# The token recurrence's diagonal and first five levels by blocks of 32 tokens instead of 128

## The chip, the core and the metric

The kernel runs on one core of a Trainium2 chip. The metric is the device time of one execution, in microseconds (us). The core works with several engines that run side by side and wait for one another through semaphores: TensorE (PE in the profile; its weight loads are PEld), VectorE (DVE), ScalarE (ACT), GpSimd (POOL) and SyncE (SP), which issues the transfers from memory.

## The reference, cut to what matters

Two layers work on 256 tokens of 1024 features. Each layer has a half-step feed-forward network, a mixer, a cross attention to 256 memory tokens and a second half-step feed-forward network. The mixer joins two groups of heads, and one of them is touched here, a recurrence with 4 heads of key and value dimension 128:

```python
S_t = diag(f_t) S_{t-1} + k_t i_t^T        # k_t = 1 - f_t, per head
o_t = S_t^T q_t
# the same without a state:
a[t, s] = sum_d q[t, d] * k[s, d] * prod_{s < j <= t} f[j, d]      for s <= t
o_t = sum_s a[t, s] * i_s
```

The other group, 8 heads of softmax attention with a decay (FoX), runs in the same mixer and isn't changed.

## The kernel before

Dense projections split every float32 weight into a high and a low part: a DMA brings 1 MB (`raw`), ACT casts it to the high part (`whi`, L149) and DVE subtracts to get the low part (`wlo`, L150). Seven buffers of each part are in use. PE then runs three matmuls per block of weights (L376, L377, L378). Of these, L378 is the one that reads `wlo` where the weights stream through as the stationary side.

`hgrn` computes the matrix `a` above for two tiles of 128 tokens (t = 0, 1) and 4 heads, in PSUM, as keys on the partitions by queries on the free axis. It starts with the diagonal (s = t): for each tile and head one 128 x 128 matmul of `k` with `q` (L577, tile `ad`). DVE multiplies it by the identity into the tile `A` (L579). Then come seven levels. At level `lv` queries in the right half and keys in the left half of a block of 2 * 2^lv tokens meet. `qf` holds q times the product of f from the middle of the block to t, and `k` holds k times the product from s to the middle. After every level DVE multiplies the right halves of `qf` (L612) and the left halves of `k` (L614) by block products `tots` (L618), so that the next level can use them.

Levels 0 to 4 run whole 128 x 128 matmuls, 4 heads for each of the two tiles, so 8 in a level (L604, tile `al`). They compute much that isn't wanted, and DVE takes only the positions of this level into `A` with a mask (`copy_predicated`, L625, one per tile, 4 x 128 columns). Levels 5 and 6 run only the blocks that are wanted (L598): 16 matmuls of 32 x 32 at level 5, 8 of 64 x 64 at level 6, and ACT copies the blocks into `A` (L622). Level 5 writes its blocks to partitions 0 and 64, and so uses two of the four groups of 32 columns of the array.

The matmuls of the recurrence work on float32 operands. In the trace one such matmul shows as two records.

The kernel is written as generators that hand over to each other. Each `yield` gives an estimate of TensorE's time, and a planner (`drive`) takes the next generator whose time has come. So the `fq` and `fk` projections (tile `acc`), the normalisation of the memory tokens (`mem`, `pt`), the gates of FoX (`pc`, `lf`, `fab`, `fe`, `fl`) and the levels of `hgrn` stand between each other on every engine. A scheduler then sets the final order of each engine's queue. Each queue runs in its order.

Of the kernel before, what the change touches and what calls it, by code (L numbers as in the profile page):

```python
# [17 lines left out]
P = 128  # L18
# [6 lines left out]
NT = S // P  # L25
# [20 lines left out]
def hymba_kernel(  # L46
# [13 lines left out]
    sm = ctx.enter_context(tc.tile_pool(name="sm", bufs=4))  # L60
# [18 lines left out]
    def smp(name="smp"):  # L79
        return pss.tile([P, 512], F32, name=nm(name), tag="smp")  # L80
# [101 lines left out]
    def consts_mixer():  # L182
        it = s4([P, P], I32, "it")
        ip = s4([P, P], I32, "ip")
        nc.gpsimd.iota(it, pattern=[[1, P]], base=0, channel_multiplier=0)
        nc.gpsimd.iota(ip, pattern=[[0, P]], base=0, channel_multiplier=1)
        xr = s4([P, P], I32, "xr")
        nc.vector.tensor_tensor(out=xr, in0=it, in1=ip, op=ALU.bitwise_xor)
        xf = s4([P, P], F32, "xf")
        nc.vector.tensor_copy(out=xf, in_=xr)  # L190
        tf = s4([P, P], F32, "tf")
        nc.vector.tensor_copy(out=tf, in_=it)
        pf = s4([P, P], F32, "pf")
        nc.vector.tensor_copy(out=pf, in_=ip)
        up = s4([P, P], F32, "up")
        nc.vector.tensor_tensor(out=up, in0=tf, in1=pf, op=ALU.is_gt)
        nc.vector.tensor_tensor(out=xf, in0=xf, in1=up, op=ALU.mult)
        masks = cp.tile([P, 5, P], U32, name="masks")
        prev = s4([P, P], F32, "ge")
        nc.vector.tensor_scalar(out=prev, in0=xf, scalar1=1.0, scalar2=None, op0=ALU.is_ge)  # L200
        for lv in range(5):
            ge = s4([P, P], F32, "ge")
            nc.vector.tensor_scalar(out=ge, in0=xf, scalar1=float(2 << lv), scalar2=None, op0=ALU.is_ge)
            nc.vector.tensor_tensor(out=masks[:, lv, :], in0=prev, in1=ge, op=ALU.subtract)
            prev = ge
        tri = cp.tile([P, NT, S], F32, name="tri")
        nc.vector.memset(tri[:, 0, :], 1.0)
        nc.vector.memset(tri[:, 1, 0:P], 0.0)
        for t in range(NT):
            nc.vector.tensor_tensor(out=tri[:, t, t * P:(t + 1) * P], in0=tf, in1=pf, op=ALU.is_ge)  # L210
        cmask = cp.tile([P, S], F32, name="cmask")
        nc.vector.memset(cmask[:, 0:P], 0.0)
        nc.vector.tensor_scalar(out=cmask[:, P:S], in0=up, scalar1=NEG, scalar2=None, op0=ALU.mult)


        ge = small(4, "gesel", bufs=2)
        pm = small(1, "pm", bufs=1)
        nc.vector.tensor_scalar(out=pm, in0=pf[:, 0:1], scalar1=64.0, scalar2=-64.0, op0=ALU.is_ge, op1=ALU.mult)
        nc.vector.tensor_tensor(out=pm, in0=pm, in1=pf[:, 0:1], op=ALU.add)
        for j, v in enumerate((8.0, 16.0, 24.0, 32.0)):  # L220
            nc.vector.tensor_scalar(out=ge[:, j:j + 1], in0=pm, scalar1=v, scalar2=None, op0=ALU.is_ge)
        sel = cp.tile([P, 6], F32, name="sel")

        nc.vector.tensor_scalar(out=sel[:, 0:1], in0=ge[:, 0:1], scalar1=-1.0, scalar2=1.0, op0=ALU.mult, op1=ALU.add)
        nc.vector.tensor_tensor(out=sel[:, 1:2], in0=ge[:, 0:1], in1=ge[:, 1:2], op=ALU.subtract)
        nc.vector.tensor_tensor(out=sel[:, 2:3], in0=ge[:, 1:2], in1=ge[:, 3:4], op=ALU.subtract)
        nc.vector.tensor_tensor(out=sel[:, 3:4], in0=ge[:, 2:3], in1=ge[:, 1:2], op=ALU.subtract)
        nc.vector.tensor_tensor(out=sel[:, 4:5], in0=ge[:, 3:4], in1=ge[:, 2:3], op=ALU.subtract)
        nc.vector.tensor_scalar(out=sel[:, 5:6], in0=ge[:, 1:2], scalar1=-1.0, scalar2=1.0, op0=ALU.mult, op1=ALU.add)
        dif = small(8, "dif")  # L230
        nc.vector.tensor_scalar(out=dif, in0=tf[:, 0:8], scalar1=pm, scalar2=-1.0, op0=ALU.subtract, op1=ALU.mult)
        oh = cp.tile([P, 8], F32, name="oh")
        nc.vector.tensor_scalar(out=oh, in0=dif, scalar1=0.0, scalar2=None, op0=ALU.is_equal)
        for v in (8.0, 16.0, 24.0):
            nc.vector.scalar_tensor_tensor(out=oh, in0=dif, scalar=v, in1=oh, op0=ALU.is_equal, op1=ALU.add)
        return masks, tri, cmask, sel, oh


    lbs = cp.tile([P, DEPTH, 4], F32, name="lbs")
# [327 lines left out]

    def hgrn(q, f, k, v, gw, oT, masks, ready, done):
        yield ready
        A2 = s4([P, NT, 4, P], F32, "A")  # L570
        A = [A2[:, t] for t in range(NT)]
        qf = s4([P, 4, S], F32, "qf")
        nc.vector.tensor_tensor(out=qf, in0=q, in1=f, op=ALU.mult)
        for t in range(NT):
            ps = smp("ad")
            for h in range(4):
                nc.tensor.matmul(ps[:, h * P:(h + 1) * P], lhsT=k[:, h, t * P:(t + 1) * P],  # L577
                                 rhs=q[:, h, t * P:(t + 1) * P], start=True, stop=True)
            nc.vector.tensor_tensor(out=A[t], in0=ps.rearrange("p (h t) -> p h t", h=4),  # L579
                                    in1=ident.unsqueeze(1).to_broadcast([P, 4, P]), op=ALU.mult)  # L580
        yield 8 * 0.213
        tots = s4([P, 1024], F32, "tots")
        tot = f.rearrange("p h t -> p (h t)")
        qflat = qf.rearrange("p h t -> p (h t)")
        kflat = k.rearrange("p h t -> p (h t)")
        for lv in range(7):
            hb = 1 << lv
            pss_ = []
            blk = lv >= 5
            if blk:  # L590
                ps = smp("al")
                pss_.append(ps)
                for t in range(NT):
                    for h in range(4):
                        c0 = (4 * t + h) * hb
                        for s0 in range(0, P, 2 * hb):
                            a = t * P + s0
                            nc.tensor.matmul(ps[s0:s0 + hb, c0:c0 + hb], lhsT=k[:, h, a:a + hb],  # L598
                                             rhs=qf[:, h, a + hb:a + 2 * hb], start=True, stop=True)
            else:  # L600
                for t in range(NT):
                    ps = smp("al")
                    for h in range(4):
                        nc.tensor.matmul(ps[:, h * P:(h + 1) * P], lhsT=k[:, h, t * P:(t + 1) * P],  # L604
                                         rhs=qf[:, h, t * P:(t + 1) * P], start=True, stop=True)
                    pss_.append(ps)
            nb = 4 * S // (2 * hb)
            tv = tot.rearrange("p (b two) -> p b two", two=2)
            qv = qflat.rearrange("p (b two j) -> p b two j", two=2, j=hb)
            kv = kflat.rearrange("p (b two j) -> p b two j", two=2, j=hb)  # L610
            with tc.high_priority(offset=HP):
                nc.vector.tensor_tensor(out=qv[:, :, 1, :], in0=qv[:, :, 1, :],  # L612
                                        in1=tv[:, :, 0:1].to_broadcast([P, nb, hb]), op=ALU.mult)
                nc.vector.tensor_tensor(out=kv[:, :, 0, :], in0=kv[:, :, 0, :],  # L614
                                        in1=tv[:, :, 1:2].to_broadcast([P, nb, hb]), op=ALU.mult)
                if lv < 6:
                    nt_ = tots[:, 1024 - 2 * nb:1024 - nb]
                    nc.vector.tensor_tensor(out=nt_, in0=tv[:, :, 0], in1=tv[:, :, 1], op=ALU.mult)  # L618
                    tot = nt_
            if blk:  # L620
                for s0 in range(0, P, 2 * hb):
                    nc.scalar.copy(out=A2[s0:s0 + hb, :, :, s0 + hb:s0 + 2 * hb],  # L622
                                   in_=pss_[0][s0:s0 + hb, 0:8 * hb].rearrange("p (t h j) -> p t h j", t=NT, h=4))
            for t in range(0 if blk else NT):
                nc.vector.copy_predicated(A[t], masks[:, lv, :].unsqueeze(1).to_broadcast([P, 4, P]),  # L625
                                          pss_[t].rearrange("p (h t) -> p h t", h=4))
            yield 8 * 0.107 if blk else 8 * 0.213
            yield (LAT_LVL,)
        ps = smp("ax")
        for h in range(4):  # L630
# [385 lines left out]
```

## Time and profile before

| what | value |
|---|---|
| median of 3 runs | 1259.83 us (1258.87 to 1261.07) |
| profiled execution | 1260.18 us, its span 1258.4 us |
| granted TensorE clock | 0.998 of full |
| PE busy | 1232.6 us (98%) |
| DVE busy | 767.4 us (61%) |
| ACT busy | 624.3 us (50%) |
| POOL busy | 36.3 us (3%) |
| DMA | 221.20 MB, 51.5% of 16 engines' span on the main queue |

Busy time of matmuls counts the length of their pipeline, so a busy PE can still be faster or slower. What tells the cost of a matmul is the step from its start to the start of the next. The stretch in which the levels run is about 256 to 296 us in the first layer, and 617 us later in the second one.

### The profile page before, as it was taken

What the parts mean: (1) busy time and instruction counts of PE and PEld (TensorE: products, weight loads), DVE (VectorE), ACT (ScalarE), POOL (GpSimd) and SP (SyncE); (2) the same over time, 40 slices, a digit from 0 to 9 for tenths busy, and PEclk for the clock granted to TensorE, in tenths of its full rate; (3) what the DMA queues carried; (4) which work ended last, traced back from release to release, by engine and by line L of the source; (5) the groups of instructions that cost most, each with busy time, mean ns of one, the idle gap of its engine ahead of it and who ended that gap; (6) DMA issues with size and microseconds to landing.
All of it is one profiled execution on the core that took longest, in us unless ns stands there. A gap on an engine that the chain in (4) does not pass through costs nothing.

```text
span 1258.4 us, 20147 instructions
## 1 busy us (share of the span) xinstructions
PE 1232.6 (98%) x8393; PEld 1129.2 (90%) x8393; DVE 767.4 (61%) x1117; ACT 624.3 (50%) x927; POOL 36.3 (3%) x50
## 2 busy tenths in 40 slices
PE   5999999999999999999999999999999999999997
PEld 4999988999889889998889998889998898899986
DVE  6554646597865674555474554476886766645643
ACT  5544434556854463444354454265485644544531
POOL 0000000002000000000000000000020000000000
PEclk9999999999999999999999999999999999999999
DMA  8654754635345264556474556465343634555640
GB/s 269 219 201 140 252 181 154 229 92 197 128 173 185 101 223 162 199 172 218 148 239 146 201 185 217 135 218 202 118 139 131 220 117 145 173 201 168 234 167 34
DMA packets 100748, 221.20 MB, mean 176 GB/s; under 512 B 4136, under 2 KB 16688, under 8 KB 100656
## 3 DMA queue, kind: packets, MB, share of 16 engines
q1 hardware_dynamic: 100656, 219.90, 51.5%
q8 instruction: 66, 1.08, 0.3%
q14 instruction: 26, 0.21, 0.1%
HBM read 218.84 MB, written 1.05 MB: 175 GB/s over the span
## 4 chain that ended last, share of the span: by engine, by line
PE 87%; ACT 4%; DVE 4%; DMA 2%; issue 1%; POOL 0%; SPq 0%; POOLq 0%; DVEq 0%; ACTq 0%
PE acc L376 27%; PE acc L377 27%; PE acc L378 27%; DVE wlo L150 2%; DMA mem<-in_mem_dram 1%; PE pt L297 1%; ACT whi L149 1%; ACT pp L711 1%; ACT fqs L727 1%; DMA raw<-in_ffn_w_gate_dram 1%; PE al L604 1%; ACT fks L729 1%; ACT fks L728 0%; POOL mrs L278 0%; PE cpo L377 0%
## 5 line engine op out<-in xcount | busy, mean ns | idle before, releaser
L150 DVE TENSOR_TENSOR wlo<-raw,whi 128x1024 fp32r<-128x1024 f32 x400 | 479.3, 1224 | 323.2 <-ACT whi L149 321.9
L149 ACT CAST whi<-raw 128x1024 fp32r<-128x1024 f32 x400 | 406.5, 1047 | 340.8 <-PE acc L378 180.3
L376 PE MATMUL acc<-xfh,whi 128*128 128x256 f32 x1536 | 433.8, 282 | 0.0
L377 PE MATMUL acc<-xfl,whi 128*128 128x256 f32 x1536 | 431.4, 281 | 0.0
L378 PE MATMUL acc<-xfh,wlo 128*128 128x256 f32 x1536 | 429.3, 280 | 0.0
L377 PEld LDWEIGHTS acc<-xfl,whi 128*128 128x128 f32 x1536 | 290.3, 189 | 0.4
L378 PEld LDWEIGHTS acc<-xfh,wlo 128*128 128x128 f32 x1536 | 289.8, 189 | 0.0
L376 PEld LDWEIGHTS acc<-xfh,whi 128*128 128x128 f32 x1536 | 288.7, 188 | 0.6
L376 PE MATMUL acc<-whi,hth 128*128 128x512 f32 x352 | 138.6, 394 | 0.0
L377 PE MATMUL acc<-wlo,hth 128*128 128x512 f32 x352 | 138.5, 393 | 0.0
L378 PE MATMUL acc<-whi,htl 128*128 128x512 f32 x352 | 138.1, 392 | 0.0
L376 PE MATMUL acc<-whi,xfh 128*128 128x512 f32 (+1 forms) x256 | 94.8, 371 | 1.6 <-ACT xfh L303 1.6
L377 PE MATMUL acc<-wlo,xfh 128*128 128x512 f32 (+1 forms) x256 | 93.9, 367 | 0.0
L378 PE MATMUL acc<-whi,xfl 128*128 128x512 f32 (+1 forms) x256 | 93.8, 366 | 0.0
L378 PEld LDWEIGHTS acc<-whi,htl 128*128 128x128 f32 x352 | 66.2, 188 | 15.1
L376 PEld LDWEIGHTS acc<-whi,hth 128*128 128x128 f32 x352 | 66.1, 188 | 14.9
L377 PEld LDWEIGHTS acc<-wlo,hth 128*128 128x128 f32 x352 | 66.1, 188 | 14.8
L376 PEld LDWEIGHTS acc<-whi,xfh 128*128 128x128 f32 x256 | 48.4, 189 | 10.0 <-ACT xfh L303 2.0
L378 PEld LDWEIGHTS acc<-whi,xfl 128*128 128x128 f32 x256 | 48.3, 188 | 8.8 <-DVE xfl L304 0.6
L284 ACT ACTIVATE jk<-xs 128x512 f32<-128x512 f32 x36 | 21.7, 603 | 68.5 <-DVE xs L478 66.4
L377 PEld LDWEIGHTS acc<-wlo,xfh 128*128 128x128 f32 x256 | 48.3, 189 | 7.8
L303 ACT CAST hth<-sil 128x512 fp32r<-128x512 f32 x36 | 22.3, 621 | 62.2 <-DVE sil L552 62.2
(226 smaller groups left out, 1373.7 us busy)
## 6 DMA issues: line engine op xcount, KB each, us to landing
raw<-in_ffn_w_down_dram SPq DMA_DIRECT2D x44, 1024.0 KB, 4.9
raw<-in_ffn_w_up_dram SPq DMA_DIRECT2D x40, 1024.0 KB, 5.5
raw<-in_ffn_w_gate_dram SPq DMA_DIRECT2D x38, 1024.0 KB, 5.2
raw<-in_w_in_dram SPq DMA_DIRECT2D x24, 1024.0 KB, 5.3
raw<-in_cross_wk_dram SPq DMA_DIRECT2D x8, 1024.0 KB, 6.0
raw<-in_w_out_dram SPq DMA_DIRECT2D x8, 1024.0 KB, 4.9
raw<-in_cross_wv_dram SPq DMA_DIRECT2D x8, 1024.0 KB, 5.1
raw<-in_cross_wq_dram SPq DMA_DIRECT2D x8, 1024.0 KB, 5.5
```

Source lines behind the costliest of these rows:

```text
L149: nc.scalar.copy(out=hi[:, :kk * cw], in_=sl)
L150: nc.vector.tensor_tensor(out=lo[:, :kk * cw], in0=sl, in1=hi[:, :kk * cw].bitcast(F32), op=ALU.subtract)
L284: nc.scalar.activation(dst, half(src, j), AF.Square, scale=1.0 / 32.0, accum_out=ss[:, j:j + 1])
L297: nc.tensor.transpose(pt[:, j * P:(j + 1) * P], hn[:, kt * P:(kt + 1) * P], ident)
L303: nc.scalar.copy(out=hi, in_=src)
L376: nc.tensor.matmul(ps, lhsT=lh, rhs=rh, start=start, stop=False)
L377: nc.tensor.matmul(ps, lhsT=lh, rhs=rl, start=False, stop=False)
L378: nc.tensor.matmul(ps, lhsT=ll, rhs=rh, start=False, stop=stop)
L604: nc.tensor.matmul(ps[:, h * P:(h + 1) * P], lhsT=k[:, h, t * P:(t + 1) * P], rhs=qf[:, h, t * P:(t + 1) * P], start=True, stop=True)
L711: nc.scalar.activation(dst, src, AF.Exp, bias=nmx[:, t:t + 1], scale=scale, accum_out=sms[:, t:t + 1])
L727: nc.scalar.copy(out=qs[own, :, sub, :], in_=qv.unsqueeze(1).to_broadcast([64, 2, S]))
L729: nc.scalar.copy(out=ks[oth, 0, sub, :], in_=kv)
```

## The change

The diagonal and the levels 0 to 4 are computed in blocks of 32 tokens. A helper `blocks` runs, for each tile and head, four matmuls of 128 x 32 keys by 32 queries, which write to partitions 0, 32, 64 and 96: 32 matmuls for the diagonal and 32 for each of the levels 0 to 4. Levels 5 and 6 use the same helper with the same matmuls as before. All 32 blocks lie in 256 columns of one PSUM tile. DVE masks them into a compact tile `Ac` of 8 x 32 columns, one instruction a level in place of two of twice the width. After level 4 ACT copies `Ac` into `A` in four pieces, and since the rest of `A` isn't written by DVE any longer, POOL clears `A` at the start (`memset`). The masks are built for 32 columns, and the estimates in the `yield`s are new: 1.3 in place of 8 * 0.213 for the diagonal and the levels 0 to 4, and 0.8 in place of 8 * 0.107 for levels 5 and 6. Lines of the first part move by 4 and those behind `hgrn` by 2.

```diff
-        masks = cp.tile([P, 5, P], U32, name="masks")
...
+        eye = cp.tile([P, 32], F32, name="eye")
+        nc.vector.tensor_scalar(out=eye, in0=xb[:, 1, :], scalar1=0.0, scalar2=None, op0=ALU.is_equal)
...
+        masks = cp.tile([P, 5, 32], U32, name="masks")
...
         A2 = s4([P, NT, 4, P], F32, "A")
         A = [A2[:, t] for t in range(NT)]
+        nc.gpsimd.memset(A2, 0.0)
+        Ac = sm.tile([P, 8, 32], F32, name=nm("Ac"), tag="Ac", bufs=1)
...
-        for t in range(NT):
-            ps = smp("ad")
-            for h in range(4):
-                nc.tensor.matmul(ps[:, h * P:(h + 1) * P], lhsT=k[:, h, t * P:(t + 1) * P],
-                                 rhs=q[:, h, t * P:(t + 1) * P], start=True, stop=True)
-            nc.vector.tensor_tensor(out=A[t], in0=ps.rearrange("p (h t) -> p h t", h=4),
-                                    in1=ident.unsqueeze(1).to_broadcast([P, 4, P]), op=ALU.mult)
-        yield 8 * 0.213
+        def blocks(ps, rhs, hb, step):
+
+            for t in range(NT):
+                for h in range(4):
+                    c0 = (4 * t + h) * hb
+                    for s0 in range(0, P, hb + step):
+                        a = t * P + s0
+                        nc.tensor.matmul(ps[s0:s0 + hb, c0:c0 + hb], lhsT=k[:, h, a:a + hb],
+                                         rhs=rhs[:, h, a + step:a + step + hb], start=True, stop=True)
+
+        ps = smp("ad")
+        blocks(ps, q, 32, 0)
+        nc.vector.tensor_tensor(out=Ac, in0=ps[:, 0:256].rearrange("p (g t) -> p g t", g=8),
+                                in1=eye.unsqueeze(1).to_broadcast([P, 8, 32]), op=ALU.mult)
+        yield 1.3
...
+            ps = smp("al")
+            blocks(ps, qf, max(32, hb), hb if lv >= 5 else 0)
...
-            for t in range(0 if blk else NT):
-                nc.vector.copy_predicated(A[t], masks[:, lv, :].unsqueeze(1).to_broadcast([P, 4, P]),
-                                          pss_[t].rearrange("p (h t) -> p h t", h=4))
-            yield 8 * 0.107 if blk else 8 * 0.213
+            else:
+                nc.vector.copy_predicated(Ac, masks[:, lv, :].unsqueeze(1).to_broadcast([P, 8, 32]),
+                                          ps[:, 0:256].rearrange("p (g t) -> p g t", g=8))
+            if lv == 4:
+                for s0 in range(0, P, 32):
+                    nc.scalar.copy(out=A2[s0:s0 + 32, :, :, s0:s0 + 32],
+                                   in_=Ac[s0:s0 + 32].rearrange("p (t h) j -> p t h j", t=NT))
+            yield 1.3 if lv < 5 else 0.8
```

The order of the queues changes only around the levels, in the same way in both layers, and SP's queue stays as it is. On PE, before, the `fq` projection of the first layer (tile `acc_2538`) stands after the diagonal and level 0. Its fourth pair of weight buffers, `whi_2524` and `wlo_2525`, is read here, and level 1 (`al_2578`, then `al_2583`) comes only after 30 of these matmuls:

```order
L378 MATMUL acc_2538<-xfh_1883,wlo_2521 128x256
L376 MATMUL acc_2538<-xfh_1883,whi_2524 128x256
L377 MATMUL acc_2538<-xfl_1884,whi_2524 128x256
L378 MATMUL acc_2538<-xfh_1883,wlo_2525 128x256
L376 MATMUL acc_2538<-xfh_1883,whi_2524 128x256
L377 MATMUL acc_2538<-xfl_1884,whi_2524 128x256
L378 MATMUL acc_2538<-xfh_1883,wlo_2525 128x256
...
L378 MATMUL acc_2538<-xfh_1881,wlo_2449 128x256
L604 MATMUL al_2578<-qf_2481,kk_2132 128x128 x4
L604 MATMUL al_2583<-qf_2481,kk_2132 128x128 x4
```

In the changed program the same place on PE has other buffer numbers (`whi_2569` and `wlo_2570` are the fourth pair, `al_2623` is level 1, whose helper's line is L589; L382 is the old L378):

```order
L382 MATMUL acc_2583<-xfh_1882,wlo_2566 128x256
L380 MATMUL acc_2583<-xfh_1882,whi_2569 128x256
L381 MATMUL acc_2583<-xfl_1883,whi_2569 128x256
L589 MATMUL al_2623<-qf_2482,kk_2131 32x32 x17
L382 MATMUL acc_2583<-xfh_1882,wlo_2570 128x256
L380 MATMUL acc_2583<-xfh_1882,whi_2569 128x256
...
L382 MATMUL acc_2583<-xfh_1880,wlo_2448 128x256
L589 MATMUL al_2623<-qf_2482,kk_2131 32x32 x15
L380 MATMUL acc_2583<-xfh_1880,whi_2451 128x256
```

Level 1 begins 10 matmuls earlier, after 20 of the projection, and is cut in two parts of 17 and 15 blocks, with 10 projection matmuls between them. The first reader of `wlo_2570` stands right behind the first part.

On DVE, before, the subtraction that makes `wlo_2525` stands ahead of the diagonal's mask and of the products that level 1 waits for:

```order
L291 TENSOR_SCALAR mem_2414<-mem_2414,mrs_2422 128x512 x2
L839 TENSOR_TENSOR zb_2381<-acc_2382,fb_1953 128x8
L839 TENSOR_TENSOR zb_2381<-acc_2383,fb_1953 128x8
L150 TENSOR_TENSOR wlo_2525<-raw_2384,whi_2524 128x1024
L579 TENSOR_TENSOR A_2480<-ad_2483,ident 128x512
L618 TENSOR_TENSOR tots_2495<-fg_2131 128x512
L579 TENSOR_TENSOR A_2480<-ad_2489,ident 128x512
L612 TENSOR_TENSOR qf_2481<-qf_2481,fg_2131 128x512
L614 TENSOR_TENSOR kk_2132<-kk_2132,fg_2131 128x512
L618 TENSOR_TENSOR tots_2495<-tots_2495 128x256
```

And the same place on DVE in the changed program, from the same normalisation of the memory tokens (`mem`) on:

```order
L295 TENSOR_SCALAR mem_2413<-mem_2413,mrs_2421 128x512 x2
L616 TENSOR_TENSOR tots_2518<-fg_2130 128x512
L594 TENSOR_TENSOR Ac_2481<-ad_2484,eye 128x256
L616 TENSOR_TENSOR tots_2518<-tots_2518 128x256
L841 TENSOR_TENSOR zb_2380<-acc_2381,fb_1952 128x8
L841 TENSOR_TENSOR zb_2380<-acc_2382,fb_1952 128x8
L610 TENSOR_TENSOR qf_2482<-qf_2482,fg_2130 128x512
L612 TENSOR_TENSOR kk_2131<-kk_2131,fg_2130 128x512
L623 COPY_PREDICATED Ac_2481<-masks,al_2519 128x256
L150 TENSOR_TENSOR wlo_2570<-raw_2383,whi_2569 128x1024
L150 TENSOR_TENSOR wlo_2576<-raw_2445,whi_2575 128x1024
L150 TENSOR_TENSOR wlo_2580<-raw_2445,whi_2579 128x1024
```

The subtraction for the fourth pair, now `wlo_2570`, has moved behind the products for level 1 and behind the mask of level 0.

## Rows read from the trace of the kernel before

**Rows 1.** The page: busy time of each engine, and the last chain by engine.

```profile
PE 1232.6 (98%) x8393; PEld 1129.2 (90%) x8393; DVE 767.4 (61%) x1117; ACT 624.3 (50%) x927; POOL 36.3 (3%) x50
...
PE 87%; ACT 4%; DVE 4%; DMA 2%; issue 1%; POOL 0%; SPq 0%; POOLq 0%; DVEq 0%; ACTq 0%
```

**Rows 2.** Busy by stretch: us, PE, PEld, DVE, ACT, POOL, PEclk, DMA, GB/s.

```profile
255.00:304.00 49.00, 48.51 (x446) 47.82 (x445) 41.91 (x75) 23.58 (x47) 4.79 (x7) 1.00 0.43 143
873.00:921.50 48.50, 47.82 (x441) 47.13 (x440) 41.41 (x74) 23.16 (x47) 4.73 (x7) 1.00 0.43 143
```

**Rows 3.** Timeline of PE, diagonal and level 0 (start us, length us, engine, line).

```profile
255.97 0.28 PE L378 MATMUL acc<-whi,xfl 128*128 128x260 f32 x1
256.09 1.95 PE L577 MATMUL ad<-hq,kk 128*128 128x128 f32 x16
257.87 1.95 PE L604 MATMUL al<-qf,kk 128*128 128x128 f32 x16
...
259.90 0.29 PE L378 MATMUL acc<-xfh,wlo 128*128 128x256 f32 x1
```

**Rows 4.** Timeline of PE, levels 5 and 6 of the first layer.

```profile
284.89 0.28 PE L378 MATMUL acc<-xfh,wlo 128*128 128x256 f32 x1
285.10 0.70 PE L598 MATMUL al<-qf,kk 128*32 128x32 f32 x32
...
286.07 0.28 PE L378 MATMUL acc<-xfh,wlo 128*128 128x256 f32 x1
...
289.26 0.28 PE L378 MATMUL acc<-xfh,wlo 128*128 128x256 f32 x1
289.46 1.15 PE L598 MATMUL al<-qf,kk 128*64 128x64 f32 x16
...
290.88 0.28 PE L378 MATMUL acc<-xfh,wlo 128*128 128x256 f32 x1
```

**Rows 5.** The same, narrow windows: the last record of each of the two bursts.

```profile
285.61 0.20 PE L598 MATMUL al<-qf,kk 128*32 128x32 f32 x1
...
290.39 0.22 PE L598 MATMUL al<-qf,kk 128*64 128x64 f32 x1
```

**Rows 6.** Timeline of DVE, first layer, from the product q * f on.

```profile
255.88 1.22 DVE L573 TENSOR_TENSOR qf<-hq,fg 128x1024 f32<-128x1024 f32 x1
...
258.33 0.23 DVE L839 TENSOR_TENSOR zb<-acc,fb 128x8 f32<-128x8 f32 x2
258.48 1.22 DVE L150 TENSOR_TENSOR wlo<-raw,whi 128x1024 fp32r<-128x1024 f32 x1
259.61 0.69 DVE L579 TENSOR_TENSOR A<-ad,ident 128x512 f32<-128x512 f32 x1
...
262.01 0.69 DVE L614 TENSOR_TENSOR kk<-kk,fg 128x512 f32<-128x512 f32 x1
262.61 0.42 DVE L618 TENSOR_TENSOR tots<-tots 128x256 f32<-128x256 f32 x1
262.95 1.35 DVE L625 COPY_PREDICATED A<-masks,al 128x512 f32<-128x512 uint32 x2
...
270.53 0.50 DVE L684 SCALAR_TENSOR_TENSOR lf<-zb,fl 128x128 f32<-128x128 f32 x2
```

**Rows 7.** Timeline of ACT, first layer: gates of FoX, and a wait further on.

```profile
268.06 0.21 ACT L679 ACTIVATE fe<-fab 128x16 f32<-128x16 f32 x1 [7.59 <-DVE fab L677]
268.18 0.58 ACT L789 ACTIVATE fq<-acc 128x512 f32<-128x512 f32 x1
268.78 1.28 ACT L681 ACT_TABLE_LOAD   x1
...
286.05 1.05 ACT L149 CAST whi<-raw 128x1024 fp32r<-128x1024 f32 x1 [4.63 <-DMA raw<-in_cross_wk_dram]
```

**Rows 8.** Timeline of PE, first layer: the matmul that waits for the gates.

```profile
270.98 1.10 PE L690 MATMUL pc<-tri,lf 128*128 128x256 f32 x4 [0.49 <-DVE lf L684]
```

**Rows 9.** The chain that ended last, where the levels have ended.

```profile
303.65 0.45 PE hot L664 x4
```

More of the change, by code (lines that the diff above doesn't have):

```diff
@@ L186, in consts_mixer @@
         nc.gpsimd.iota(ip, pattern=[[0, P]], base=0, channel_multiplier=1)
[L187 to L190, printed above, removed]
         tf = s4([P, P], F32, "tf")
@@ L196, in consts_mixer @@
         nc.vector.tensor_tensor(out=up, in0=tf, in1=pf, op=ALU.is_gt)
-        nc.vector.tensor_tensor(out=xf, in0=xf, in1=up, op=ALU.mult)
-        masks = cp.tile([P, 5, P], U32, name="masks")
-        prev = s4([P, P], F32, "ge")
-        nc.vector.tensor_scalar(out=prev, in0=xf, scalar1=1.0, scalar2=None, op0=ALU.is_ge)
+        xi = s4([P, 2, 32], I32, "xi")
+        nc.vector.tensor_scalar(out=xi[:, 0, :], in0=ip[:, 0:32], scalar1=31, scalar2=None, op0=ALU.bitwise_and)
+        nc.vector.tensor_tensor(out=xi[:, 1, :], in0=it[:, 0:32], in1=xi[:, 0, :], op=ALU.bitwise_xor)
+        xb = s4([P, 3, 32], F32, "xb")
+        nc.vector.tensor_copy(out=xb[:, 0:2, :], in_=xi)
+        nc.vector.tensor_tensor(out=xb[:, 2, :], in0=tf[:, 0:32], in1=xb[:, 0, :], op=ALU.is_gt)
+        eye = cp.tile([P, 32], F32, name="eye")
+        nc.vector.tensor_scalar(out=eye, in0=xb[:, 1, :], scalar1=0.0, scalar2=None, op0=ALU.is_equal)
+        xf = xb[:, 1, :]
+        nc.vector.tensor_tensor(out=xf, in0=xf, in1=xb[:, 2, :], op=ALU.mult)
+        masks = cp.tile([P, 5, 32], U32, name="masks")
+        ges = s4([P, 6, 32], F32, "ge")
+        for lv in range(6):
+            nc.vector.tensor_scalar(out=ges[:, lv, :], in0=xf, scalar1=float(1 << lv), scalar2=None, op0=ALU.is_ge)
         for lv in range(5):
[L202 to L205, printed above, removed]
+            nc.vector.tensor_tensor(out=masks[:, lv, :], in0=ges[:, lv, :], in1=ges[:, lv + 1, :], op=ALU.subtract)
         tri = cp.tile([P, NT, S], F32, name="tri")
@@ L235, in consts_mixer @@
             nc.vector.scalar_tensor_tensor(out=oh, in0=dif, scalar=v, in1=oh, op0=ALU.is_equal, op1=ALU.add)
-        return masks, tri, cmask, sel, oh
+        return (masks, eye), tri, cmask, sel, oh
     lbs = cp.tile([P, DEPTH, 4], F32, name="lbs")
@@ L569, in hgrn @@
         yield ready
+        masks, eye = masks
         A2 = s4([P, NT, 4, P], F32, "A")
         A = [A2[:, t] for t in range(NT)]
+        nc.gpsimd.memset(A2, 0.0)
+        Ac = sm.tile([P, 8, 32], F32, name=nm("Ac"), tag="Ac", bufs=1)
         qf = s4([P, 4, S], F32, "qf")
         nc.vector.tensor_tensor(out=qf, in0=q, in1=f, op=ALU.mult)
-        for t in range(NT):
-            ps = smp("ad")
-            for h in range(4):
-                nc.tensor.matmul(ps[:, h * P:(h + 1) * P], lhsT=k[:, h, t * P:(t + 1) * P],
-                                 rhs=q[:, h, t * P:(t + 1) * P], start=True, stop=True)
-            nc.vector.tensor_tensor(out=A[t], in0=ps.rearrange("p (h t) -> p h t", h=4),
-                                    in1=ident.unsqueeze(1).to_broadcast([P, 4, P]), op=ALU.mult)
-        yield 8 * 0.213
+        def blocks(ps, rhs, hb, step):
[11 more added lines that the diff above has]
+        yield 1.3
         tots = s4([P, 1024], F32, "tots")
@@ L587, in hgrn @@
             hb = 1 << lv
[L588 to L606, printed above, removed]
+            ps = smp("al")
+            blocks(ps, qf, max(32, hb), hb if lv >= 5 else 0)
             nb = 4 * S // (2 * hb)
@@ L619, in hgrn @@
                     tot = nt_
-            if blk:
+            if lv >= 5:
                 for s0 in range(0, P, 2 * hb):
                     nc.scalar.copy(out=A2[s0:s0 + hb, :, :, s0 + hb:s0 + 2 * hb],
-                                   in_=pss_[0][s0:s0 + hb, 0:8 * hb].rearrange("p (t h j) -> p t h j", t=NT, h=4))
-            for t in range(0 if blk else NT):
-                nc.vector.copy_predicated(A[t], masks[:, lv, :].unsqueeze(1).to_broadcast([P, 4, P]),
-                                          pss_[t].rearrange("p (h t) -> p h t", h=4))
-            yield 8 * 0.107 if blk else 8 * 0.213
+                                   in_=ps[s0:s0 + hb, 0:8 * hb].rearrange("p (t h j) -> p t h j", t=NT, h=4))
+            else:
[6 more added lines that the diff above has]
+            yield 1.3 if lv < 5 else 0.8
             yield (LAT_LVL,)
```

## The prediction

> **What bounds the kernel now.** I read the page first. PE is busy for 98% of the span and 87% of the last chain is PE [rows 1], so what counts is PE's own work and the few places where it stands. In the stretch of the levels PE is busy for 48.51 of 49.00 us, with DVE at 41.91, ACT at 23.58 and POOL at 4.79, and the second layer shows the same [rows 2]. So I work out the first layer and double it. The timeline of PE then gives the price of a burst of small matmuls, and the timelines of DVE and ACT tell whether PE, if it comes earlier, finds its operands.
>
> **What the PE work costs.** A projection matmul takes a step of 0.118 us: between the third one after level 5 (286.07) and the last before level 6 (289.26) there are 27 steps [rows 4]. The price of a burst is the time between the projection matmuls around it less their own three steps (0.35). The diagonal and level 0 together take 259.90 - 255.97 - 0.35 = 3.58 us [rows 3], so a whole level of 8 matmuls takes 1.79. Level 5 takes 286.07 - 284.89 - 0.35 = 0.83 for 16 blocks of 32, and level 6 takes 1.27 for 8 blocks of 64 [rows 4].
>
> Within a burst the starts tell the pace: 16 records of 128 columns in 1.78 us, 0.111 each [rows 3]; 64 columns (290.39 - 289.46) / 15 = 0.062; 32 columns (285.61 - 285.10) / 31 = 0.0165 [rows 4, 5]. The first two lie on a line that would give about 0.037 for 32 columns, so the 32-column records ran at more than twice the pace that their width alone explains. Level 5 writes two groups of columns of the array, 0 and 64, in turn, and I read this as two groups at work side by side, each at about 0.033. What is left of a burst's price is fixed: 0.83 - 32 * 0.0165 = 0.30, and 1.27 - 16 * 0.062 = 0.28 for level 6.
>
> The change replaces 8 matmuls by 32, so 16 records by 64, in each of six bursts, and these go to four groups of columns in turn. No row shows four groups. If all four work side by side, the pace halves to 0.0083 and a level costs 0.30 + 0.53 = 0.83. If only two ever do, the pace stays at 0.0165 and a level costs 1.36. If a burst of neighbouring groups has no overlap, it is 0.033 and 2.41. I take 0.83, since the nearest row (level 5) shows two groups that don't slow each other at all, and keep the others for the range and the rivals.
>
> A rule of the Trainium skill speaks against this change: "TensorEngine Tiling (Array Packing)", section Instruction Overhead, says that each matmul has about 60 cycles of overhead, so that a free size of 1 lasts as long as one of 60, and warns against shrinking a dimension that is small already. By it 64 records of 25 ns and the fixed 0.30 would make 1.9 us a level by estimate, more than 1.79, and nothing would be won. The trace differs where it can be seen: 32 columns went at 16.5 ns in level 5. The same page's tables have four tiles at 32 columns and up to 4 times the speed, which would give the 0.83.
>
> Per layer PE's work goes from 6 * 1.79 = 10.7 to 1.36 (diagonal and level 0 as one burst, 0.30 + 1.06) + 1.13 (level 1, cut in two, so the fixed part twice) + 3 * 0.83 = 5.0. That would be 5.7 us a layer, but not all of it reaches the end.
>
> **What PE then waits for.** The order moves two things together: level 1 begins after 20 projection matmuls instead of 30, and the subtraction of the fourth weight pair goes behind level 1's products on DVE. I follow both queues in the first layer. Until the product q * f, DVE's queue is as before.
> - PE: the diagonal takes the slot at 256.09 and ends at 256.77. Level 0 needs q * f, which ends at 255.88 + 1.22 = 257.10 [rows 6]: a wait of 0.3. It ends at 257.78 and 20 projection matmuls last to 260.14.
> - DVE comes free of the memory tokens at 258.33 [rows 6]. Then `tots` of 512 columns (0.60, the step from one such product to the next, 262.01 to 262.61), the new mask of 256 columns (0.34, the step of the 256-wide `tots`), `tots` (0.34), `zb` (0.15), `qf` (0.60), `kk` (0.69): level 1's keys are ready at 261.05. PE stands for 0.9.
> - The first 17 blocks of level 1 take 0.58, to 261.63. DVE masks level 0 (half of a 0.62 step plus a little, say 0.36) and then makes the fourth low half, 1.22 [rows 6], ready at 262.54. PE stands for 0.9 again. Behind it in PE's queue are 10 projection matmuls (1.18), the other 15 blocks (0.55), 30 matmuls (3.54), level 2 (0.83) and 3 more (0.35): PE arrives at the matmul of the FoX gates (`pc`) at 268.99.
> - `pc` needs `lf`, and that needs ACT: `fq`, whose projection is complete at 266.67, then 0.60 for it, 1.28 for the table load and 0.21 for the logarithm [rows 7], so 268.76, and 0.45 from the start of `lf` to `pc` as before (270.53 to 270.98) [rows 6, 8]: 269.2.
>
> Before, `pc` started at 270.98 after a wait of 0.49 [rows 8], with 3 projection matmuls fewer done. The lead there is 270.98 - 269.2 + 0.35 = 2.1 us. Of the 5.7 us the waits ahead of it thus eat 1.7. From there on levels 3 and 4 give 2 * 0.96 = 1.9. DVE keeps up: it loses 4 * 0.3 us of diagonal masks and 10 masks of 0.62 for 5 of 0.36 over both parts, and by the same steps the keys of levels 2, 3 and 4 are ready 0.5 to 1.5 us before PE asks, by estimate. If that margin were gone, it would cost its lack, some tenths a level.
>
> **What I cost at nothing.** POOL's clearing of `A` stands ahead of the memory tokens' inverse root, on an engine that is idle for nine tenths of the stretch [rows 2], and its buffer has been free since the feed-forward network. ACT's four copies of `Ac`, some 0.36 each (the estimate for a 256-column step), fall where ACT stood for 4.63 us waiting for a transfer [rows 7]; if that cover is gone, 1.5 us a layer are at risk, since the output product reads `A`. The transfers are triggered by DVE's subtractions, which come earlier too. The constants are built once, in a stretch where DVE has room: between nothing and a gain of a few tenths.
>
> **The sum.** 2.1 + 1.9 = 4.0 us a layer, 8.0 in all. After the levels the chain goes from PE's transposes at 303.65 to ACT [rows 9], so what follows starts from PE's end and moves with it. The profiled execution took 1260.18 us (span 1258.4 and 1.8 around it), 0.35 above the median; from the median, 1259.83 - 8.0 = **1251.8 us**.
>
> **The rivals.**
> - Only two column groups overlap. The same chain with 0.0165 a record: PE leaves level 0 at 258.51, waits 0.2 for the keys and 0.6 for the weights, reaches `pc` at 269.77 without a wait; lead 1.21 + 0.35, then 2 * 0.43: 2.4 us a layer, **1255.0 us**. For it: two is all that any row shows. Against: the two groups of level 5 are free of each other. Chance 0.27.
> - Small records don't overlap in the long bursts (128 records against 32 in level 5, and neighbouring groups): 0.033 a record. Level 0 ends at 260.61, `pc` comes at 273.16, 1.8 us late, and levels 3 and 4 lose 0.62 each: 3.1 us a layer, **1266 us**, slower. It decides from the pace at which a level costs 1.79 again, (1.79 - 0.30) / 64 = 0.0233. Against it: the steady pace of level 5 [rows 4, 5]. Chance 0.05. The rule of the Trainium skill on the overhead ("TensorEngine Tiling (Array Packing)", Instruction Overhead) lies just past that point.
> - The lead is given back. ACT and DVE carry the FoX softmax behind the levels, and if ACT comes late with the copies and casts, PE waits there for what it won: 1.5 to 4 us a layer lost, **1257 to 1260 us**. For it: ACT gets 8 copies more. Against: it was busy for under half of the stretch [rows 2]. Chance 0.08.
>
> The forecast has 0.57, with its own range 1250.3 to 1253.3. The other 0.03 is for surprises. What this kernel's measurement can tell from no change is about 0.2%, 2.5 us. The first two cases and the better half of the third are faster by more: 0.86. Same 0.09, slower 0.05. The range reaches from a slightly better chain (1249.9) past the two-group case (1256.2).
>
> **What the profile of the changed kernel would show.** Bursts of 64 records whose starts lie 8 ns apart if I am right, 16 in the first rival, over 23 in the second; about 0.8 us between the projection matmuls around levels 2 to 4; PE standing about 0.9 us ahead of level 1 and as much before the fourth pair of weights; `pc` at about 269.2 us in the first layer and the end of the levels 4 us earlier. PE waiting longer between 303 and 345 us would show the third rival. A pace between 8 and 16 ns, or a wait for the fourth weight pair that is much longer than 0.9, would make the size wrong.

## The result and the profile after

The changed kernel takes 1252.39 us (median of 4, 1251.2 to 1254.4) against 1260.12 us (median of 4): a ratio of 0.9938, 95% interval 0.9926 to 0.9951. The forecast was 1251.8. The profiled execution is the slowest of the four, 1254.4 us with a span of 1252.6.

The page of the changed kernel, which answers to [rows 1]: PE's work is 7.2 us shorter with 576 records more, DVE's 8.8 us shorter, ACT's 4.1 longer.

```profile
PE 1225.4 (98%) x8969; PEld 1118.6 (89%) x8969; DVE 758.6 (61%) x1108; ACT 628.4 (50%) x935; POOL 38.2 (3%) x52
...
PE 90%; ACT 4%; DVE 3%; DMA 1%; issue 1%; POOL 0%; SPq 0%; POOLq 0%; DVEq 0%; ACTq 0%
```

The timeline of PE, which answers to [rows 3, 8]: diagonal, levels 0 to 2, and the gates' matmul.

```profile
256.91 0.76 PE L589 MATMUL ad<-hq,kk 128*32 128x32 f32 x64
258.09 0.76 PE L589 MATMUL al<-qf,kk 128*32 128x32 f32 x64 [0.42 <-DVE qf L580]
262.03 0.50 PE L589 MATMUL al<-qf,kk 128*32 128x32 f32 x34 [0.62 <-DVE kk L612]
264.86 0.45 PE L589 MATMUL al<-qf,kk 128*32 128x32 f32 x30
268.80 0.28 PE L382 MATMUL acc<-xfh,wlo 128*128 128x256 f32 x1
269.01 0.76 PE L589 MATMUL al<-qf,kk 128*32 128x32 f32 x64
270.05 0.28 PE L382 MATMUL acc<-xfh,wlo 128*128 128x256 f32 x1
270.27 1.10 PE L692 MATMUL pc<-tri,lf 128*128 128x256 f32 x4
```

A burst is 0.76 long by its row, and its last record 0.20 [rows 5], so 63 steps take 0.56: 8.9 ns a record. Level 2 costs 270.05 - 268.80 - 0.35 = 0.90. The waits of PE in the first layer's stretch, 255 to 304 us, are the three that were forecast ahead of `pc`, and none at `pc`:

```profile
PE acc L382 <- DVE wlo L150: 1.0, 1, 1.0
PE al L589 <- DVE kk L612: 0.6, 1, 0.6
PE al L589 <- DVE qf L580: 0.4, 1, 0.4
```

In the second layer (866 to 921 us) only the first two of them come, 1.0 and 0.6: there PE doesn't wait for `qf`.

On DVE and ACT (timelines, answering to [rows 6, 7]) the chain of the gates ends just as PE arrives; ACT's casts, which stood 4.63 us for a transfer before, now stand 1.24, and the four copies of `Ac` follow:

```profile
269.83 0.49 DVE L686 SCALAR_TENSOR_TENSOR lf<-zb,fl 128x128 f32<-128x128 f32 x2 [0.71 <-ACT fl L683]
```

```profile
280.92 1.05 ACT L149 CAST whi<-raw 128x1024 fp32r<-128x1024 f32 x1 [1.24 <-DMA raw<-in_cross_wk_dram]
281.95 1.65 ACT L627 COPY A<-Ac 32x256 f32<-32x256 f32 x4
```

**A ruler.** From the start of the diagonal to the start of the last row of transposes of the output (`hot`) is a layer's stretch, and what lies between the two layers' stretches is 569.5 us before and 569.8 in every other profile. So the two stretches show each kernel's gain free of the start, which matters: the first diagonal starts at 256.09 us before, and between 255.9 and 257.3 us in five profiles (after, after_again, e_serial, e_pairs, e_dve2) whose queues don't differ up to there. I worked them out from the starts in PE's timeline:

| kernel | layer 1, us | layer 2, us | median time, us |
|---|---|---|---|
| before | 47.84 | 48.03 | 1260.1 to 1260.3 |
| after | 44.09 | 44.96 | 1252.39 |
| after, second profile (after_again) | 44.35 | 43.52 | 1252.87 |
| e_serial | 48.31 | 48.30 | 1261.64 |
| e_pairs | 45.02 | 44.61 | 1254.51 |
| e_dve2 | 45.70 | 45.04 | 1256.04 |
| e_wlo | 46.63 | 45.09 | 1258.47 |
| e_wlo_gates | 43.72 | 43.03 | 1252.17 |
| e_gates_early | 42.06 | 42.41 | 1249.06 |

Layer 2 of the first profile was odd: 0.87 us longer than layer 1. The busy time by stretch (columns as in [rows 2]) shows why. PE's granted clock fell there, first in the kernel after, then in the second profile of the same kernel, where it did not:

```profile
870.00:880.00 10.00, 8.41 (x232) 7.63 (x231) 9.00 (x17) 3.68 (x5) 1.46 (x1) 0.86 0.36 104
880.00:890.00 10.00, 10.00 (x193) 9.40 (x192) 8.36 (x21) 4.66 (x8) 0.00 (x0) 0.96 0.21 61
```

```profile
870.00:880.00 10.00, 8.57 (x241) 7.81 (x240) 9.56 (x18) 4.37 (x6) 1.46 (x1) 1.00 0.31 108
880.00:890.00 10.00, 10.00 (x197) 9.40 (x195) 9.13 (x22) 5.42 (x9) 0.00 (x0) 1.00 0.29 81
```

After PE had stood for keys and weights it ran at the lower level, 1.2 GHz, for some 3.4 us (windows of 1 us show a clock of 0.65, 0.50, 0.50 and 0.65 from 877 to 881 us): projection records came 0.21 apart instead of 0.118. This layer is 44.96 - 43.52 = 1.4 us longer than the same layer of the second profile, and the other three executions, at a mean clock of 0.999 against its 0.997, took 1251.2 to 1252.4.

### The profile page after: what moved, and what is told of

Read it like the earlier page. It is cut to its first block, busy times and chain, and to the rows that moved or that the text cites. A ratio compares the mean times of both kernels' runs of the same rounds, so it can differ in the third digit from the quotient of the medians.

```text
span 1252.6 us, 21298 instructions
## 1 busy us (share of the span) xinstructions
PE 1225.4 (98%) x8969; PEld 1118.6 (89%) x8969; DVE 758.6 (61%) x1108; ACT 628.4 (50%) x935; POOL 38.2 (3%) x52
## 4 chain that ended last, share of the span: by engine, by line
PE 90%; ACT 4%; DVE 3%; DMA 1%; issue 1%; POOL 0%; SPq 0%; POOLq 0%; DVEq 0%; ACTq 0%
PE acc L380 28%; PE acc L381 28%; PE acc L382 28%; PE pt L301 1%; ACT whi L149 1%; DVE wlo L150 1%; ACT pp L713 1%; ACT fqs L729 1%; DMA mem<-in_mem_dram 1%; PE al L589 1%; DMA raw<-in_ffn_w_gate_dram 1%; ACT fks L731 1%; ACT fks L730 0%; POOL mrs L282 0%; PE cpo L381 0%
## 5 line engine op out<-in xcount | busy, mean ns | idle before, releaser
L382 PE MATMUL acc<-xfh,wlo 128*128 128x256 f32 x1536 | 430.0, 280 | 1.9 <-DVE wlo L150 1.9
L382 PEld LDWEIGHTS acc<-xfh,wlo 128*128 128x128 f32 x1536 | 290.4, 189 | 2.2 <-DVE wlo L150 2.2
L382 PE MATMUL acc<-whi,htl 128*128 128x512 f32 x352 | 138.1, 392 | 0.0
L382 PE MATMUL acc<-whi,xfl 128*128 128x512 f32 (+1 forms) x256 | 94.2, 368 | 0.0
L382 PEld LDWEIGHTS acc<-whi,htl 128*128 128x128 f32 x352 | 66.2, 188 | 15.1
L382 PEld LDWEIGHTS acc<-whi,xfl 128*128 128x128 f32 x256 | 48.6, 190 | 8.9 <-DVE xfl L308 0.6
```

Of the source, the lines that this page charges most:

```text
L382: nc.tensor.matmul(ps, lhsT=ll, rhs=rh, start=False, stop=stop)
```

## The experiments

**Is it the side by side of the column groups?** Two kernels issue the same 32 blocks in other orders: e_serial one column group after another, e_pairs groups 0 and 64 first and then 32 and 96. The edit is e_serial's; e_pairs has `[(0, 64), (32, 96)]` as its last list.

```diff
-            for t in range(NT):
-                for h in range(4):
-                    c0 = (4 * t + h) * hb
-                    for s0 in range(0, P, hb + step):
...
+            heads = [range(0, P, hb + step)] if hb + step > 32 else [(s0,) for s0 in range(0, P, 32)]
+            for group in heads:
+                for t in range(NT):
+                    for h in range(4):
+                        c0 = (4 * t + h) * hb
+                        for s0 in group:
...
```

> The same blocks as the changed kernel, but in each burst of the diagonal and the levels 0 to 4 first all blocks of one group of 32 columns, then all of the next; the number of instructions is the same. Theory (the gain comes from the four column groups working side by side): a burst of 64 records goes at 0.033 us a record instead of 0.009, so about 2.1 us instead of 0.57, a level costs about 2.4 us, and the time is 1262 to 1266 us, slower than the kernel before. Rival (a record of 32 columns costs a fixed issue time, whatever group it writes): 0.009 a record as in the changed kernel, 1252.4 us.

> The same blocks as the changed kernel, but in each burst first those of the column groups 0 and 64 in turn, then those of 32 and 96. Theory (as many groups work side by side as follow each other in the order): 0.0165 us a record, a burst of 64 takes 1.05 us, a level 1.36, and the time is 1254.5 to 1256 us. Rival (issue sets the pace): 0.009 a record and 1252.4 us.

e_serial took 1261.64 us (1260.98 to 1262.76), ratio 1.0012 [1.0002, 1.0021]; e_pairs 1254.51 (1254.08 to 1255.04), ratio 0.9956 [0.9941, 0.9971], as the theory had it. Level 2's burst in the timeline of PE, e_serial first, then e_pairs:

```profile
269.23 1.91 PE L591 MATMUL al<-qf,kk 128*32 128x32 f32 x64
```

```profile
268.09 1.11 PE L591 MATMUL al<-qf,kk 128*32 128x32 f32 x64
```

By the same working as above the pace is (1.91 - 0.20) / 63 = 27 ns, (1.11 - 0.20) / 63 = 14 ns, and 8.9 ns in the order of the kernel. The same instructions on the same data, with every engine's queue outside the bursts as in the changed kernel (only level 1 is cut after 11 and 13 blocks in place of 17), and the whole gain depends on the order of a loop. e_pairs is the prediction's first rival built on purpose, and came within 0.5 us of its 1255.0. e_serial ended just under its range (1262 to 1266), since its pace was 27 ns and not 33.

**Can the waits be won back?** e_wlo lets the scheduler put the fourth weight pair's low half ahead of level 1's products; level 1 then stays whole behind 30 projection matmuls. The edit raises every such subtraction of the kernel; what lies between the layers' stretches stays at 569.8 us.

```diff
-                nc.vector.tensor_tensor(out=lo[:, :kk * cw], in0=sl,
-                                        in1=hi[:, :kk * cw].bitcast(F32), op=ALU.subtract)
+                with tc.high_priority(offset=50):
+                    nc.vector.tensor_tensor(out=lo[:, :kk * cw], in0=sl,
+                                            in1=hi[:, :kk * cw].bitcast(F32), op=ALU.subtract)
```

> The changed kernel, with the subtraction that makes the low half of the weights raised in priority: in both layers the fourth pair is made ahead of level 1's products, and level 1 comes whole, after 30 projection matmuls. PE then stands neither ahead of level 1 nor at the fourth weight pair (0.55 and 0.93 us a layer in the changed kernel), and one burst less is opened. Theory (two chains are about level: PE's own and the one of the FoX gates over DVE and ACT, which sets when the gates' matmul can start): the wait moves to the gates' matmul, about 2 us a layer, and the time falls by 0.3 to 1.5 us in all, 1251 to 1252 us. Rival (PE's two waits are all that stands between): 1.8 us a layer are won, 1248.8 us.

Both expectations missed: 1258.47 us (1255.45 to 1260.22), ratio 0.9984 [0.9975, 0.9994]. The two waits were gone and the wait moved to `pc`, as the theory had it, but it was 2.7 and 3.3 us in the two layers in place of 2. The gates' bias add (`zb`) now stood later on DVE, ACT behind it, and PE at `pc`. Rows of DVE, ACT and PE from e_wlo's timeline:

```profile
270.33 0.49 DVE L687 SCALAR_TENSOR_TENSOR lf<-zb,fl 128x128 f32<-128x128 f32 x2 [1.98 <-ACT fl L684]
```

```profile
266.12 0.64 ACT L843 COPY fv<-acc 128x252 f32<-128x252 f32 x2 [8.40 <-DVE zb L842]
```

```profile
270.77 0.46 PE L693 MATMUL pc<-tri,lf 128*128 128x256 f32 x1 [2.73 <-DVE lf L687]
```

And PE's clock fell behind that stand in the first layer (columns as in [rows 2]):

```profile
270.00:272.00 2.00, 1.23 (x5) 1.06 (x5) 1.67 (x5) 0.29 (x2) 0.00 (x0) 0.80 0.00 0
272.00:274.00 2.00, 2.00 (x10) 1.91 (x10) 1.46 (x5) 0.37 (x1) 0.00 (x0) 0.50 0.00 0
274.00:276.00 2.00, 2.00 (x52) 1.86 (x53) 1.04 (x3) 0.96 (x2) 0.00 (x0) 0.85 0.00 0
```

The ten executions follow their mean granted clock: those at 0.995 took 1259.6 to 1260.2, at 0.996 1258.3 to 1258.7, at 0.997 and above 1255.5 to 1256.8.

e_wlo_gates is e_wlo with the gates' matmul further back, behind level 4:

```diff
-LAT_Q, LAT_G1, LAT_G2, LAT_M = 5.0, 9.0, 2.0, 18.0
+LAT_Q, LAT_G1, LAT_G2, LAT_M = 5.0, 17.0, 2.0, 18.0
```

> As the one before, and the gates' matmul of FoX is moved behind level 4 by a longer planned latency of its operands, 17 in place of 9 us; nothing between needs it. Theory (the gates' chain held the one before back): now no wait is left around the levels, PE does 5.6 us less work a layer than before, and the time falls by 3 to 4 us against the changed kernel, to 1248.5 to 1249.5 us. Rival (the wait goes on to the next level, whose keys DVE makes): no more than 1 us, 1251.5 us.

1252.17 us (1250.8 to 1253.05), ratio 0.9935 [0.9919, 0.9952]: the wait at `pc` is gone, the clock stays up, but the rival was right. DVE's queue still held the log gate, 1.98 us late for ACT, ahead of the next level's products, so the wait went to level 3. From the waits of PE, 255 to 304 us:

```profile
PE al L590 <- DVE kk L613: 1.4, 1, 1.4
```

e_gates_early also moves the gates' first two operations forward on DVE, `zb` ahead of level 0's products and the absolute value right behind them:

```diff
-        nc.vector.scalar_tensor_tensor(out=ab, in0=zb, scalar=-1.0, in1=zb, op0=ALU.mult, op1=ALU.max)
+        with tc.high_priority(offset=60):
+            nc.vector.scalar_tensor_tensor(out=ab, in0=zb, scalar=-1.0, in1=zb, op0=ALU.mult, op1=ALU.max)
...
-            nc.vector.tensor_tensor(out=zb[:, t, :], in0=ps[t][:, 252:260], in1=fb, op=ALU.add)
+            with tc.high_priority(offset=60):
+                nc.vector.tensor_tensor(out=zb[:, t, :], in0=ps[t][:, 252:260], in1=fb, op=ALU.add)
```

> The kernel after with three places in the order changed: the fourth weight pair's low half ahead of level 1's products on DVE (as in e_wlo), the gates' matmul behind level 4 (as in e_wlo_gates), and the gates' bias add and absolute value ahead of level 0's products on DVE, so that ACT's two gate activations are done before DVE comes to the log gate and DVE does not stand 1.98 us there. Theory (what is left to win in e_wlo_gates is that stand, which made level 3 wait 1.4 us for its keys): both waits of a layer gone, 1.2 to 1.5 us a layer below e_wlo_gates' 1252.2: 1249 to 1250 us, and no wait over 0.5 us between the diagonal and level 5. Rival (DVE is full from q*f to level 2 whatever its order, so the wait only goes on to another level): within 0.7 us of e_wlo_gates, 1251.5 to 1252.5.

1249.06 us (1247.91 to 1250.44), ratio 0.9909 [0.9893, 0.9926], as the theory had it, and faster than both kernels. The log gate no longer waits, and one wait of PE is left in the first layer's stretch; in the second layer the same wait, at level 0 for `qf`, is 0.8 us, more than the 0.5 expected. DVE's row first, then PE's waits:

```profile
266.37 0.49 DVE L688 SCALAR_TENSOR_TENSOR lf<-zb,fl 128x128 f32<-128x128 f32 x2
```

```profile
PE al L590 <- DVE qf L581: 0.5, 1, 0.5
```

> The version with the gates early once more, beside e_burst2_apart on one chip, 1248 to 1250.5 us, both waits of a layer gone as before.

Beside other kernels: 1248.86 us (1248.74 to 1249.61), ratio 0.9911 [0.9896, 0.9926].

**The kernel after once more.**

> The kernel after, unchanged, beside the others on one chip: 1251 to 1254 us. Theory (the half clock of 3.4 us in its second layer came by chance in that execution, 1.2 to 2 us): a profile without it ends near 1250.5 to 1251 and shows about 3.8 us won in each layer. Rival (it comes each time at the same place, after the two stands of level 1): the same 1.2 GHz stretch near 877 to 881 us again, span 1252.6.

1252.87 us (1252.0 to 1253.98), ratio 0.994 [0.9925, 0.9955]. The fall of the clock did not come again, so it doesn't come each time at this place; the two layers won 3.5 and 4.5 us, and not 3.8 each. The span, 1251.9, was 0.9 above the range expected.

**DVE's part of the gain.** Two kernels issue each masked copy of the five levels twice: e_dve2 on the kernel after, e_early_dve2 on e_gates_early.

```diff
                 nc.vector.copy_predicated(Ac, masks[:, lv, :].unsqueeze(1).to_broadcast([P, 8, 32]),
                                           ps[:, 0:256].rearrange("p (g t) -> p g t", g=8))
+                nc.vector.copy_predicated(Ac, masks[:, lv, :].unsqueeze(1).to_broadcast([P, 8, 32]),
+                                          ps[:, 0:256].rearrange("p (g t) -> p g t", g=8))
```

> The kernel after with the masked copy of each of the five first levels issued twice, so that DVE has about its load of before in the levels (5 x 0.36 us a layer more) while PE's order and bursts stay. Theory (the gain is PE's burst price, and DVE's share of it is small because only level 1's keys and the gates wait for DVE): 0.3 to 1.5 us above the kernel after. Rival (the gain comes from DVE being lighter): most of the 8 us back, 1257 to 1260.

> e_gates_early with the masked copy of each of the five first levels issued twice, as e_dve2 did on the kernel after (where it cost 3.2 us, and PE stood 1.5 us a layer at the gates' matmul for the log gate). Here the log gate lies ahead of the second copies and the gates' matmul behind level 4. Theory (a copy's time on DVE counts only through the gates' chain): 0 to 1 us above e_gates_early's 1249.06, 1249 to 1250. Rival (DVE, nearly full between 257 and 272 us, passes its load on to PE wherever it lies, through the keys of the next level): 1251 to 1253.

e_dve2 took 1256.04 us, 3.2 above the kernel after on the same chip: twice what I expected, and under the rival. Nearly all of it is one new wait, 1.5 us in each layer, PE at `pc` for the log gate:

```profile
PE pc L694 <- DVE lf L688: 1.5, 1, 1.5
```

But the time of the copies didn't make this wait. The order of ACT's queue changed with them. In the kernel after, the gates' first activation (`fe`) stands ahead of `fq`, and its table was loaded 5 us before (261.40); in e_dve2 `fq` stands ahead of `fe`, so a table load of 1.28 us falls between `fq` and `fe`, and a second one ahead of the logarithm (`fl`). ACT's timeline in the kernel after, then in e_dve2:

```profile
267.04 0.22 ACT L681 ACTIVATE fe<-fab 128x16 f32<-128x16 f32 x1 [4.36 <-DVE fab L679]
267.67 0.60 ACT L791 ACTIVATE fq<-acc 128x512 f32<-128x512 f32 x1 [0.42 <-PE acc L382]
268.29 1.28 ACT L683 ACT_TABLE_LOAD   x1
269.58 0.22 ACT L683 ACTIVATE fl<-fe 128x16 f32<-128x16 f32 x1
```

```profile
268.02 0.60 ACT L793 ACTIVATE fq<-acc 128x512 f32<-128x512 f32 x1 [6.29 <-PE acc L382]
268.64 1.28 ACT L683 ACT_TABLE_LOAD   x1
269.93 0.22 ACT L683 ACTIVATE fe<-fab 128x16 f32<-128x16 f32 x1
270.17 1.28 ACT L685 ACT_TABLE_LOAD   x1
271.46 0.22 ACT L685 ACTIVATE fl<-fe 128x16 f32<-128x16 f32 x1
```

From the start of `fq` to that of `fl` it takes 1.91 us in the one and 3.44 in the other, 1.53 more, which is the wait. The second layer shows the same order (`fq` at 882.86, `fl` at 886.29, 3.43). DVE had `fab` ready at 267.69, ahead of `fq`. In the old order, by estimate, `fl` would have come at 269.93 and `pc` 0.7 later, at 270.6, which is when PE came to it: no wait. So e_dve2 doesn't tell what a masked copy costs. Nor does it bring back the load of before: by the steps of the rows (0.62 for a mask of before, 0.60 for a diagonal's, 0.34 for a new one) the masks took 7.4 us a layer on DVE before and 2.0 after, and the second copies add 1.7.

e_early_dve2, where the gates have room and ACT's gate activations keep their order, took 1250.15 (1249.16 to 1250.95), just over its range and 1.1 above e_gates_early; in its profile the two stretches came to 84.5 us, as in e_gates_early, so the copies cost nothing that the stretches show. With the whole load of before on DVE no kernel was run.

**Fixed part and records.** e_burst2 issues each burst of 32 blocks twice, on e_gates_early; e_burst2_apart does so in levels 2 to 4 only.

```diff
-            for t in range(NT):
+            for t in 2 * list(range(NT)) if step == 0 else range(NT):
```

> e_gates_early with every burst of 32 products (diagonal and levels 0 to 4) issued twice in a row into the same bank, so 64 records become 128. Theory (a burst is a fixed part of some 0.35 us, paid once where PE goes over to the small tiles and back, and 9 ns a record): each burst 0.55 to 0.6 us longer, some 3.4 us a layer less what lies in the 0.7 us stand ahead of level 0, 1254.5 to 1256.5. Rival (no fixed part: the 0.9 us are 64 records of 14 ns): each burst 0.9 us longer, 1258.5 to 1260.

> e_gates_early with the bursts of levels 2, 3 and 4 alone issued twice, which stand 4 us apart, while the diagonal and levels 0 and 1 keep their 64 records. In e_burst2 PE stood 4.0 and 3.2 us for nothing that the profile shows and the granted clock then fell to half, though each doubled burst was just 0.53 us longer. Theory (PE ran out of instructions there: they come in blocks of 16 KB, one at a time, and the diagonal with level 0 alone took two blocks of 256 in 2.4 us): no stand of that kind here, each of the six doubled bursts 0.53 us longer, 3.2 us together, 1252.3 (1251.5 to 1253). Rival (a burst of 128 small products is itself the trouble, wherever it stands): stands of 2 to 4 us again and the half clock, 1258 or more.

A burst of 128 records is 1.30 long, 0.54 more than one of 64, so 8.4 ns for each added record, and the fixed part is the 0.90 of a level less 64 of them: 0.36. So far that is the theory. But the times were 1270.95 and 1258.57 us, past both expectations of e_burst2 and, for e_burst2_apart, where the rival had it. PE stood for nothing that the profile shows. Timelines of PE, e_burst2 first, then e_burst2_apart:

```profile
261.75 1.49 PE L590 MATMUL al<-qf,kk 128*32 128x32 f32 x93 [3.96 <-issue]
```

```profile
273.55 0.19 PE L590 MATMUL al<-qf,kk 128*32 128x32 f32 x1 [0.84 <-issue]
...
279.45 0.46 PE L590 MATMUL al<-qf,kk 128*32 128x32 f32 x31 [1.25 <-issue]
...
897.13 0.58 PE L382 MATMUL acc<-xfl,whi 128*128 128x256 f32 x1 [2.83 <-issue]
```

The page's row of the instruction queue tells what it is, in before, the kernel after, e_burst2 and e_burst2_apart:

```profile
q8 instruction: 66, 1.08, 0.3%
```

```profile
q8 instruction: 70, 1.15, 0.4%
```

```profile
q8 instruction: 76, 1.25, 0.4%
```

```profile
q8 instruction: 73, 1.20, 0.4%
```

The packets are 16 KB each and they count PE's instructions: 8393 matmuls with as many weight loads are 65.6 times 256, 8969 are 70.1, 9737 are 76.1, 9353 are 73.1. By the packets' own times in the trace PE came back 1.4 to 1.5 us after one had landed, in all eight such stands of the two kernels, as 260.26 and PE at 261.75, 272.14 and 273.55, 278.05 and 279.45, 895.76 and 897.13. They come one at a time, in e_burst2_apart at 259.0, 263.5, 267.4 and 271.2, and each level with its 30 projection matmuls there takes 316 instructions in about 5 us. So the small products have a second price beside their pace, a supply of about 256 instructions in 4 us, and the rival was right on the time but for another reason than the size of a burst: in layer 1 the first doubled burst, level 2, ran through, and in layer 2 all three did. The account closes, by estimate: in e_burst2_apart's profile the stands are 0.84 + 1.25 + 2.83 = 4.9 us, the clock was at half for 6.8 us behind the last of them, which costs up to 3.4, and six bursts are 0.53 longer, 3.2; that is 11.5, and its span is 10.7 above that of e_gates_early_again on the same chip. Before, no two packets begin closer than 10.9 us; in the kernel after the closest are 3.8 us apart (869.7 and 873.5), at the edge, but no such stand is seen there. e_wlo, with single bursts, shows a short one, 0.28 us at 261.87, 1.28 after a packet had landed.

## Why the prediction was right, point by point

- **The pace (8.3 ns, a level 0.83).** Measured 8.9 ns and 0.90. The reading of level 5 as two groups at work side by side held: one group alone goes at 27 ns, two at 14, four at 8.9. The rule of "TensorEngine Tiling (Array Packing)", Instruction Overhead, in the Trainium skill, 60 cycles for each matmul, would have made 25 ns: e_serial's 27 agrees with it, but with groups in turn that overhead runs side by side as well.
- **The waits.** Forecast 0.3, 0.9, 0.9 and 0.2 at `pc` (269.2 against an arrival at 268.99); the first layer's waits show 0.4, 0.6, 1.0 and none. The chain of the gates was to end just as PE arrives: `pc` stood at 270.27, with a start 0.82 later than before's (256.91 against 256.09), so at 269.45 against the forecast 269.2.
- **The sum.** 4.0 us a layer were forecast. The ruler gives 3.75 and 3.07 in the first profile, the second with the fall of the clock, and 3.49 and 4.51 in the second, 8.0 together. By the medians it is 7.7 and 7.5. That the two layers of the second profile add up to just the 8.0 is in part luck: I worked out the first layer and doubled it, and the first won less than 4.0 and the second more. PE's waits were 2.3 us in the first layer (0.7, 0.6 and 1.0) and 1.4 in the second, which has none for `qf`. The levels behind `pc` cost 0.07 more each than I put, and a fall of the clock goes with a layer 1.4 us longer in one of four: I had no term for it, and before's profile shows none.
- **Costed at nothing.** ACT's four copies fell into the wait for the transfer, and the stretch between the layers grew by 0.3 us only, so the lead was not given back. POOL's clearing (0.95 us) ran at 210 us, 46 ahead of the diagonal. What the constants are worth can't be told from the start of the diagonal, which differs by 1.4 us from profile to profile.
- **What stays open.** "DVE keeps up" held: behind `pc` PE waits for nothing of DVE's in the levels. What the lighter masks are worth isn't shown. e_serial has them too and wins nothing, so alone they bring nothing there; e_early_dve2 takes a third of their saving back and its stretches don't grow; e_dve2's loss belongs to the order of ACT's queue. What it does show is how narrow the chain of the gates is: in the kernel after it ends at `pc` as PE arrives, so 1.5 us more on ACT were 1.5 us more of PE's time.

## What to carry to other kernels

Small matmuls that fill different column groups of the array run side by side only where neighbouring instructions change the group, so look at the innermost loop before counting instructions. When PE becomes faster, follow the queue of the engine that feeds it and the chain of each side task (here the gates): a reordering that removes one wait can move it, as here twice, and paid only when the last of the chain was moved too. Compare the order of every engine's queue before you put a time down to an edit: here a second copy on DVE turned two activations round on ACT. And count PE's instructions per microsecond in a dense burst: here their supply was a limit of its own, about 256 in 4 us.

## What the runs showed of the hardware that was not expected

- **Instruction supply.** 16 KB packets of 256 instructions, PE back 1.4 to 1.5 us after a packet has landed, stands of up to 4.0 us (e_burst2). The Trainium skill ("Runtime: NRT & Kernel Launch", Instruction fetch mechanics) has the blocks of 16 KiB and 256 instructions, as the counts here show, and calls the cost of crossing one mostly hidden; with 128 records of 8.7 ns in a row these traces differ.
- **The clock.** The granted clock fell to 1.2 GHz for some microseconds behind PE's stands of 4.0, 2.2 and 3.2 us in e_burst2, 2.8 in e_burst2_apart and 2.7 in e_wlo's first layer, but not behind the 3.3 us in the second layer of the same e_wlo execution. Behind the 0.6 and 1.0 us of the kernel after it fell in one of four layers profiled, behind the 1.5 us of e_dve2 and the 1.4 of e_wlo_gates in none. What decides it these runs do not settle.
